# Two attention units share one PSUM tile of two banks, one split per engine and one transpose

## The chip, the core and the metric

The kernel runs on one NeuronCore of a Trainium2 chip. The core has a matrix engine (TensorE, PE in the profile, with its weight loads shown apart as PEld), three engines for elementwise work (VectorE or DVE, ScalarE or ACT, GpSimd or POOL), and SyncE (SP), whose queue issues nearly all DMAs here. Each engine works through its own queue in order and waits at an instruction whose inputs or buffers are not ready. Matmuls write to PSUM, which has eight banks of 512 float32 per partition; DVE and ACT read and write it too. The metric is the device time of one execution in microseconds (us).

## The reference

One layer of an encoder for a sequence of 1024 tokens with 1024 features. One projection of the input gives queries, keys, values and gates of two groups of eight heads of 64 features. Group A is attention in a 2-D neighbourhood of a grid of 16 rows and 64 columns with a learned relative bias; group B is windowed attention with rotary positions, where pairs of query heads share keys and values, and with one more logit per head, the sink. Each group's output is multiplied by SiLU of its gate, projected, added to the scaled input and normalised:

```
h = x @ w_in                                   # 1024 x 1024 by 1024 x 3328
q_a, k_a, v_a, z_a, q_b, k_b, v_b, z_b = split(h)
y_a = neighborhood_attention(q_a, k_a, v_a, rel_bias)      # window 8 x 16
y_b = windowed_gqa_with_sink(rope(q_b), rope(k_b), v_b, sink)   # |i - j| <= 128
mixed = concat(y_a * silu(z_a), y_b * silu(z_b))
x = layer_norm(alpha * x + mixed @ w_out, gain, bias)
```

All is float32 at the outside.

## The kernel before

Float32 products are made from float16 halves: an operand is scaled and split into a high part (a rounding to float16) and a low part (the rest), and three matmuls, high by high, high by low and low by high, stand for one.

The program has three stages. First the values are projected and scales are found. Then the first six of 21 column blocks of the projection run alone (`project`, line 379). In the third stage attention and the other 15 blocks run together: attention goes in steps, and between its matmuls `pump_to` gives out the waiting projection matmuls at a rate that the list `FILL_AT` sets by step. After the last step comes the output projection (`out_mms`, line 1031) and the normalisation.

Attention has 128 units, 64 of group B and then 64 of group A, each 128 queries by up to 384 keys. In group B a unit is a block of 128 queries of one head; the first and last block of a head have 256 keys, the other six 384. In group A a unit is half of the rows of one 16-column strip; its softmax covers 288 or 384 keys (an outer or an inner strip), and the two units of a strip are neighbours. In step i, in the order of the program:

- `stage_qk` (lines 816, 817, 826): two matmuls put the scores of unit i into a bank of PSUM, and one DVE operation adds the bias or mask, finds the row maximum and leaves the negated scores in one of two SBUF buffers.
- `stage_ot` and `stage_pv` (lines 901 and 881), each fourth step: for a quad, four units, probabilities by values, and the transpose of the quad's finished output. The matmuls of quad q come in step 4q + 9.
- `stage_tr` for unit i - 1 (lines 852, 853, 856): ACT writes the high half of the probabilities to an SBUF buffer `split`, DVE the low half, and one DMA issued on SP transposes up to six blocks of 128 by 128 (three blocks of keys, two halves) into a tile `tr`.
- `stage_exp` for unit i (line 842): ACT takes the exponential of the scores into the unit's bank in PSUM and sums each row.

In between, operations that wait in queues of the program's own (`enq`, `pop`: splits of weights, queries and keys, rotary positions, gates) are given out, about one a step for each engine. The order of all engines in this stage is the order in which this code emits (`manual_schedule`).

A unit's bank of PSUM is free for a later unit when the DVE split (line 853) has read it. There are four such banks, taken in turn, two for projection groups ("pj") and two for outputs ("t"). There are six `split` buffers of one unit, used in turn, and nine `tr` tiles of six blocks.

Of the kernel before, what the change touches and what calls it, by code (L numbers as in the profile page):

```python
# [7 lines left out]
F32 = mybir.dt.float32  # L8
F32R = mybir.dt.float32r
F16 = mybir.dt.float16  # L10
I32 = mybir.dt.int32
BF16 = mybir.dt.bfloat16
AF = mybir.ActivationFunctionType
ALU = mybir.AluOpType
# [10 lines left out]
PSCALE = 2.0 ** 14  # L25
MSCALE = 2.0 ** -44
QSCALE = 2.0 ** -15
LTT, LPP, BP, BH, BR, ND, NA, NX, F1 = 1, 6, 2, 9, 5, 1, 1, 6, 0.2
NSPLIT, NP = 6, 2
ORDER = ["zb0", "z0", "zb1", "kb", "qb0", "z1", "qb1", "zb2", "qb2", "k0", "qb3", "zb3", "q0", "k1", "q1",  # L30
         "k2", "q2", "z2", "k3", "q3", "z3"]
NPRO = 6
# [29 lines left out]
def hybrid_block(ctx, tc, xT, x, wt, wv, wo, bias, sink, gain, lbias, cos, sin, bmask, out):  # L62
    nc = tc.nc
    PS = bass.MemoryType.PSUM
# [4 lines left out]
    zp = ctx.enter_context(tc.tile_pool(name="zp", bufs=1))  # L69
    dram = ctx.enter_context(tc.tile_pool(name="dram", bufs=1, space=bass.MemoryType.DRAM))  # L70
    ps2 = ctx.enter_context(tc.tile_pool(name="ps2", bufs=2, space=PS))
    ps1 = ctx.enter_context(tc.tile_pool(name="ps1", bufs=1, space=PS))

    def bank(tag):
        bufs = {"pj": 2, "s": 4, "t": 2}[tag]
        return (ps1 if bufs == 1 else ps2).tile([128, 512], F32, tag=tag, name=f"ps_{tag}", bufs=bufs)

    vd = dram.tile([4, S, 256], F16, name="vd")
    vwin = [dram.tile([4, ROWS, WINW[b] * 256], F16, name=f"vwin{b}") for b in range(4)]
# [10 lines left out]
    for half in range(2):  # L90
        for k in range(KT):
            t = big_tile(f"x{half}{k}", dt=F32 if half else F32R)
# [312 lines left out]
    with ExitStack() as vctx:  # L405
# [4 lines left out]
        ps = bank("t")  # L410
# [154 lines left out]
            nc.vector.tensor_reduce(vm[:, t:t + 1], v32[t], axis=AXX, op=ALU.max, apply_absolute_value=True)  # L565

        tags = ("pj", "pj", "s", "s", "t", "t", "s", "s")
        banks = [bank(t) for t in tags]
        ordered.enter_context(tc.manual_schedule())
        first_tiles()  # L570
        interleave(load_x(0, 1), load_wv(1))
# [43 lines left out]
        ahead(2)  # L615
        v_out(banks[5], 2, 1)
        nc.vector.tensor_mul(vdq, unit[:, 0:1], unit[:, 1:2])
        part = {i: bank(tags[i]) for i in (0, 1, 2, 3, 6, 7)}
        for i, k in enumerate(KO):
            ahead(i + 3)  # L620
            if 1 <= i < 5:
# [24 lines left out]
        for a in range(2):  # L646
            ps = bank(tags[4 + a])
# [106 lines left out]
        return us  # L754

    units = unit_list()
    split = [ap.tile([128, 3, 2, 128], F16, name=f"split{i}", bufs=1) for i in range(NSPLIT)]
    sns = [ap.tile([128, 388], F32, name=f"sn{i}", bufs=1) for i in range(2)]
    for t in split:
        nc.gpsimd.memset(t, 0.0)  # L760
# [2 lines left out]
    st = {}  # L763
    on = {}

    def geom(u):
        g, p, j, t, _ = u
        if g == "a":
            b, half = t
            w = WINW[b]  # L770
            return NKEY[b], [4 * w] * 3
        lo, hi = max(t - 1, 0), min(t + 2, 8)
        return 128 * (hi - lo), [128] * (hi - lo)
# [20 lines left out]
    def stage_qk(u):  # L794
        g, p, j, t, _ = u
        n, _c = geom(u)
        ps = bank("s")
        m, end = n, 384
        if g == "a":
            b, half = t  # L800
            m, end = NROW[half] * WINW[b], 384 if half else 384 - WINW[1]
            q = stks["q", p, j][:, 512 * half + 128 * b:512 * half + 128 * b + 128]
            sl = [stks[w, p, j].rearrange("p (r c) -> p r c", c=GW)[
                :, 4 * half:4 * half + NROW[half], WIN0[b]:WIN0[b] + WINW[b]] for w in ("kh", "kl")]
            bias_t, op = st.pop((u, "b"))
            need(op)
            init = 3e38
        else:
            q = stks["q", f"b{p}", j][:, 128 * t:128 * t + 128]
            lo = max(t - 1, 0) * 128  # L810
            kv = p // 2
            sl = [stks[w, "b", kv][:, lo:lo + n] for w in ("kh", "kl")]
            bias_t = bm[:, 128 if t == 0 else 0:(128 if t == 0 else 0) + n]
            h = 2 * p + j
            init = nsk[:, h:h + 1]
        nc.tensor.matmul(ps[:, :m], q, sl[0], start=True, stop=False)  # L816
        nc.tensor.matmul(ps[:, :m], q, sl[1], start=False, stop=True)  # L817
        s0 = sns[units.index(u) % 2]
        sn = s0[:, end - m:]
        if g == "b" and t < 2:  # L820
            nc.vector.tensor_copy(s0[:, 384:385], nsk[:, h:h + 1])
        elif units.index(u) == 64:
            nc.vector.memset(s0[:, 384 - WINW[1]:384], -NEG)
        nm = ap.tile([128, 1], F32, tag="nm", name="nm", bufs=6)
        c = min(p, 1) if g == "b" else 2
        nc.vector.tensor_tensor_reduce(sn[:, :m], ps[:, :m], bias_t, sg[:, c:c + 1], init,  # L826
                                       op0=ALU.add, op1=ALU.min, accum_out=nm)
        st[u, "sn"] = sn
        st[u, "ps"] = ps
        st[u, "nm"] = nm  # L830

    def stage_exp(u):
        n, _c = geom(u)
        m = n + 1 if u[0] == "b" else n
        sn, nm = st.pop((u, "sn")), st.pop((u, "nm"))
        pt = st.pop((u, "ps"))
        k = units.index(u) % 4
        if k == 0:
            st["sm"] = ap.tile([128, 4], F32, tag="sm", name="sm", bufs=4)
        sm = st["sm"]  # L840
        st[units.index(u) // 4, "sm"] = sm
        nc.scalar.activation(pt[:, :m], sn[:, :m], AF.Exp, bias=nm, scale=-1.0, accum_out=sm[:, k:k + 1])  # L842
        st[u, "p"] = pt

    def stage_tr(u):
        g, p, j, t, _ = u
        n, ch = geom(u)
        pt = st.pop((u, "p"))
        c, m = ch[0], len(ch)
        hl = split[units.index(u) % NSPLIT]  # L850
        src = pt[:, :n].rearrange("p (k c) -> p k c", c=c)
        nc.scalar.activation(hl[:, :m, 0, :c], src, AF.Copy, scale=PSCALE)  # L852
        nc.vector.scalar_tensor_tensor(hl[:, :m, 1, :c], src, PSCALE, hl[:, :m, 0, :c],  # L853
                                       op0=ALU.mult, op1=ALU.subtract)
        tr = ap.tile([128, 6, 128], F16, tag="tr", name="tr", bufs=BH)
        nc.sync.dma_start(tr[:, :2 * m, :], hl[:, :m].rearrange("p k i c -> p (k i c)"), transpose=True)
        st[u, "tr"] = tr

    def quad(q):
        g, p, j, t, _ = units[4 * q]  # L860
# [320 lines left out]
    for i in range(-LD, NU + LO):  # L1181
        if 0 <= i + LD < NU:
            stage_load(units[i + LD], i)
        if i < 0:
            continue
        clock["step"] = i
        per, h = divmod(i, 16)
        bulk["step"] = i
        if i in VA_AT:
            gather_v(0, VA_AT.index(i))  # L1190
        for n, at_ in WO_SCAN:
            if at_ == i:
                load_ops["wo", ("s", n)] = enq("sp", lambda n=n: wo_load(n, True), wo_ops.get(WO_PREV.get(n) if n == 15 else None))
                wo_scan(n, True)
        for n in range(16):
            if WO_LD[n] == i:
                load_ops["wo", n] = enq("sp", lambda n=n: wo_load(n), wo_ops.get(WO_PREV.get(n) if n < 15 else None),
                                        wo_ops.get({9: 0, 10: 1, 12: 2, 13: 3, 14: 4, 15: 5}.get(n)),
                                        w_ops.get(17 + n if 4 <= n <= 8 else None))
                if n < 9 or n == 11:  # L1200
                    wo_scan(n)
        if i == WO_SCALE:
            wo_scale()
        for n in range(len(WO_AT)):
            if WO_AT[n] == i:
                wo_split(n)
        if i == 131:
            enq("sp", gain_load, *m_ops[4])
        if i in M_AT:
            m_queue(4 + M_AT.index(i))  # L1210
        if bulk["last"] != i or (queues["sp"] and i - queues["sp"][0].born > 2):
            pop("sp", 1 if i < 118 else 3)
        if i < NU:
            u = units[i]
            if u[3] in (0, 4):
                need(*stk_ops[f"b{u[1]}", u[2], u[3] // 4])
            if u[3] == (0, 0):
                need(*stk_ops[u[1], u[2], 0], *stk_ops[u[1], u[2], 1])
            stage_qk(u)
        q, m = divmod(i - LP - 3, 4)  # L1220
        if i >= Q30 + 2:
            q, m = (NU // 4 - 2, i - Q30 - 2) if i < Q30 + 4 else divmod(i - LP - 3, 4)
        elif i >= Q30:
            q, m = -1, 0
        if m == 0 and 0 <= q - 1 < NU // 4:
            stage_ot(q - 1)
        if m == 0 and 0 <= q < NU // 4:
            stage_pv(q)
        if i > Z3_END:
            pop("dve", 1, 0)  # L1230
        if 0 <= i - LT < NU:
            stage_tr(units[i - LT])
        pop("act", 1, 0)
        pump_to(i + F1)
        if 0 <= q < NU // 4:
            g, p, j, h = quad(q)
            if g == "a" and p < 3 and (j, h, m) in VA_STEP:
                gather_v(p + 1, VA_STEP.index((j, h, m)))
        if m == 1 and 0 <= q < NU // 4:
            stage_on(q)  # L1240
        pop("dve", ND if i < M_AT[1] else 2, same=True)
        if i < NU:
            stage_exp(units[i])
        pop("act", NA if i < M_AT[0] and len(queues["act"]) < 5 else 2)
        pop("pool", NP)
        pump_to(i + 1)
# [78 lines left out]
```

## Time and profile before

| | us |
|---|---|
| median of 3 runs | 445.71 (445.67 to 446.71) |
| the profiled execution | 446.49 |
| its span, first to last instruction | 444.7 |
| PE, DVE, ACT, POOL busy | 437.5, 344.2, 308.3, 221.6 |
| attention, first to last score matmul | 121.8 to 355.1 |

The page of the profile gives each engine's busy time, the span in 40 slices (tenths of a slice busy, in one digit), the chain of work that ended last, and groups of instructions: line, engine, operation, output and inputs, shape, count, then busy time in us and mean time of one in ns, then the idle time of the engine just before them and what ended it. In a timeline a line begins with the start and the duration in us. In a list of waits the figures are the total in us, the times, and the longest. The end of a matmul is modelled, so its shown duration is longer than the distance to the next one.

### The profile page before, as it was taken

How to read it: one execution, taken by the hardware profiler on the slowest of the kernel's cores; microseconds unless marked ns; L12 is line 12 of the kernel's file. 1: busy time of each engine (PE TensorE's matmuls, PEld its weight loads, DVE VectorE, ACT ScalarE, POOL GpSimd, SP SyncE). 2: the span in 40 equal slices, each digit the busy share in tenths (PEclk: the TensorE clock that was granted, in tenths of full speed). 3: DMA queues.
4: the chain of work that ended last, by engine and by line, in shares of the span. 5: the costliest groups of instructions: out<-in, count | busy, mean ns of one | idle time of the engine just before them, and what ended most of it. 6: DMA issues, size and time to landing. Idle time of an engine off the chain costs nothing.

```text
span 444.7 us, 9505 instructions
## 1 busy us (share of the span) xinstructions
PE 437.5 (98%) x3289; PEld 255.5 (57%) x3289; DVE 344.2 (77%) x849; ACT 308.3 (69%) x700; POOL 221.6 (50%) x235
## 2 busy tenths in 40 slices
PE   9999999999999999999999999999999999999994
PEld 8997754444445565655565655656555654444453
DVE  5978967438986898887988888888878837589944
ACT  5759789766499988887868887888778946302401
POOL 0110074646839558866506767765574405205740
PEclk9999999999999999999999999999999999999997
DMA  8921469984659999587978899998999998103612
GB/s 272 390 91 60 145 235 339 336 292 169 213 127 214 206 190 181 98 162 143 164 127 175 169 182 180 213 170 213 192 204 253 167 172 347 55 0 102 232 69 72
DMA packets 133841, 81.39 MB, mean 183 GB/s; under 512 B 101280, under 2 KB 113440, under 8 KB 133536
## 3 DMA queue, kind: packets, MB, share of 16 engines
q1 hardware_dynamic: 133648, 80.64, 75.4%
q8 instruction: 26, 0.43, 0.4%
q14 instruction: 23, 0.19, 0.2%
q10 hardware_dynamic: 144, 0.13, 0.1%
HBM read 50.34 MB, written 9.96 MB: 136 GB/s over the span
## 4 chain that ended last, share of the span: by engine, by line
PE 91%; DMA 3%; POOL 3%; DVE 1%; issue 1%; ACT 1%; SPq 0%; POOLq 0%; DVEq 0%; ACTq 0%
PE ps_pj L379 44%; PE ps_s L1031 9%; PE ps_s L486 6%; PE ps_t L881 6%; PE ps_pj L1031 5%; PE ps_t L1031 5%; PE ps_s L816 4%; PE ps_s L817 4%; PE ps_pj L486 3%; PE ps_t L486 3%; DMA bias<-in_bias 3%; PE ps_t L901 1%; POOL wl L205 1%; PE ps_t L412 1%; POOL ks L295 1%
## 5 line engine op out<-in xcount | busy, mean ns | idle before, releaser
L379 PE MATMUL ps_pj<-xf,wh 128*128 128x512 f16 x672 | 202.1, 379 | 0.1
L379 PE MATMUL ps_pj<-xf,wl 128*128 128x512 f16 x336 | 127.3, 379 | 0.0
L379 PEld LDWEIGHTS <-wh 128*128 128x128 f16 x672 | 63.7, 98 | 60.4 <-DVE ks L263 0.5
L842 ACT ACTIVATE ps_s<-sn,nm 128x385 f32<-128x385 f32 (+3 forms) x128 | 70.1, 548 | 25.1 <-DVE nm L826 24.6
L853 DVE SCALAR_TENSOR_TENSOR split<-ps_s,split 128x384 f16<-128x384 f32 (+2 forms) x128 | 65.7, 513 | 27.5 <-ACT split L852 25.9
L1031 PEld LDWEIGHTS <-m 128*128 128x128 f16 x432 | 40.0, 98 | 41.1 <-DVE m L939 0.2
L852 ACT ACTIVATE split<-ps_s 128x384 f16<-128x384 f32 (+2 forms) x128 | 57.8, 452 | 2.5 <-DMA tr<-split 0.2
L204 POOL TENSOR_SCALAR wr<-wr,wsc 128x512 f32<-128x512 f32 x26 | 20.6, 791 | 68.1 <-ACT wh L199 61.6
L379 PEld LDWEIGHTS <-wl 128*128 128x128 f16 x336 | 32.9, 98 | 37.4
L826 DVE CUSTOM_DVE_ANT_0 sn<-ps_s,bm,nsk 128x384 f32<-128x384 f32 (+1 forms) x64 | 40.7, 636 | 2.0 <-PE ps_s L817 1.7
L1031 PE MATMUL ps_s<-wo,m 128*128 128x512 f16 (+1 forms) x192 | 40.8, 366 | 0.0
L816 PE MATMUL ps_s<-ks,qs 128*128 128x384 f16 (+4 forms) x128 | 39.2, 306 | 0.3 <-DVE qs L263 0.3
L817 PE MATMUL ps_s<-ks,qs 128*128 128x384 f16 (+4 forms) x128 | 39.2, 306 | 0.0
L826 DVE CUSTOM_DVE_ANT_0 sn<-ps_s,bias,sg 128x264 f32<-128x264 f32 (+1 forms) x64 | 35.0, 547 | 4.5 <-issue 1.5
L881 PEld LDWEIGHTS <-tr 128*128 128x128 f16 (+1 forms) x1104 | 36.6, 98 | 2.2
L205 POOL TENSOR_TENSOR wl<-wr,wh 128x512 f16<-128x512 f32 x26 | 32.7, 1257 | 2.2
L788 POOL TENSOR_SCALAR bias<-bias,rsg 128x552 f32<-128x552 f32 (+1 forms) x24 | 19.1, 797 | 23.8 <-DMA bias<-in_bias 22.6
L295 POOL COPY ks<-ks 64x512 f16<-64x512 f16 x40 | 26.0, 661 | 7.1 <-DVE ks L263 2.8
L1086 ACT ACTIVATE sd<-mv,eps 128x1 f32<-128x1 f32 x8 | 2.4, 295 | 36.5 <-DVE mv L1084 35.2
L1031 PE MATMUL ps_pj<-wo,m 128*128 128x512 f16 (+1 forms) x144 | 26.2, 326 | 0.0
L1130 POOL TENSOR_TENSOR xr<-xr,gb 128x512 f32<-128x512 f32 x7 | 9.8, 1396 | 32.4 <-ACT xr L1127 32.4
L842 ACT ACTIVATION_READ_ACCUMULATOR ps_s<-sn,nm 128x1 f32 x128 | 24.4, 190 | 0.0
(188 smaller groups left out, 813.8 us busy)
## 6 DMA issues: line engine op xcount, KB each, us to landing
ws<-in_wt SPq DMA_DIRECT2D x15, 512.0 KB, 5.9
wr<-in_wt SPq DMA_DIRECT2D x26, 256.0 KB, 3.6
wor<-in_wo SPq DMA_DIRECT2D x22, 256.0 KB, 3.5
bias<-in_bias SPq DMA_DIRECT2D x16, 276.0 KB, 3.3
xr<-in_x SPq DMA_DIRECT2D x8, 512.0 KB, 9.6
out<-xr SPq DMA_DIRECT2D x15, 256.0 KB, 2.1
bias<-in_bias SPq DMA_DIRECT2D x8, 368.0 KB, 3.8
wvraw<-in_wv SPq DMA_DIRECT2D x9, 320.0 KB, 5.8
```

The costliest lines, as they stand in the source:

```text
L205: nc.gpsimd.tensor_sub(l, raw, h)
L295: nc.gpsimd.tensor_copy(t[o, sl], t[a, sl])
L379: nc.tensor.matmul(ps, a[:, k % 4, :], mv, start=(k == 0 and i == 0), stop=(k == KT - 1 and i == 2))
L486: nc.tensor.matmul(ps[:, :320], lh[:, ts], rh[:, cs], start=(k == ko[0] and i == 0), stop=(k == ko[-1] and i == 2))
L816: nc.tensor.matmul(ps[:, :m], q, sl[0], start=True, stop=False)
L817: nc.tensor.matmul(ps[:, :m], q, sl[1], start=False, stop=True)
L826: nc.vector.tensor_tensor_reduce(sn[:, :m], ps[:, :m], bias_t, sg[:, c:c + 1], init, op0=ALU.add, op1=ALU.min, accum_out=nm)
L842: nc.scalar.activation(pt[:, :m], sn[:, :m], AF.Exp, bias=nm, scale=-1.0, accum_out=sm[:, k:k + 1])
L852: nc.scalar.activation(hl[:, :m, 0, :c], src, AF.Copy, scale=PSCALE)
L853: nc.vector.scalar_tensor_tensor(hl[:, :m, 1, :c], src, PSCALE, hl[:, :m, 0, :c], op0=ALU.mult, op1=ALU.subtract)
L881: nc.tensor.matmul(ps[:, HD * m:HD * m + HD], a, b_, start=(i == 0), stop=(i == len(mms) - 1))
L1031: nc.tensor.matmul(ps, lh[:, ts], rh[:, cs], start=(e == EO[0] and i == 0), stop=(e == EO[-1] and i == 2))
```

## The change

Units are taken in pairs, 2k and 2k + 1. A pair has one PSUM tile of two banks, one for each unit, and there are two such tiles in place of four single banks. `stage_tr` runs once for a pair, in step 2k + 2, where it stood for unit 2k + 1 before. Where both units have as many keys, one ACT and one DVE operation split both; where they differ (a first or last block of a head in group B), each unit is split by an operation of its own, and the longer unit is put first. One DMA transposes all blocks of the pair, up to 12. There are three `split` buffers of two units, and four `tr` tiles of 12 blocks. Other users of the tag "s" (the projection of the values, the output projection) take halves of pair tiles.

```diff
-LTT, LPP, BP, BH, BR, ND, NA, NX, F1 = 1, 6, 2, 9, 5, 1, 1, 6, 0.2
-NSPLIT, NP = 6, 2
+LTT, LPP, BP, BH, BR, ND, NA, NX, F1 = 1, 6, 2, 4, 5, 1, 1, 6, 0.2
+NSPLIT, NP = 3, 2
...
+    halves_s = []
+
+    def pair_bank():
+        return ps2.tile([128, 2, 512], F32, tag="s", name="ps_s", bufs=2)
 
     def bank(tag):
-        bufs = {"pj": 2, "s": 4, "t": 2}[tag]
-        return (ps1 if bufs == 1 else ps2).tile([128, 512], F32, tag=tag, name=f"ps_{tag}", bufs=bufs)
+        if tag == "s":
+            if not halves_s:
+                t = pair_bank()
+                halves_s.extend((t[:, 0, :], t[:, 1, :]))
+            return halves_s.pop(0)
+        return ps2.tile([128, 512], F32, tag=tag, name=f"ps_{tag}", bufs=2)
...
-        banks = [bank(t) for t in tags]
+        banks = {i: bank(tags[i]) for i in (0, 1, 2, 6, 3, 7, 4, 5)}
...
-        part = {i: bank(tags[i]) for i in (0, 1, 2, 3, 6, 7)}
+        part = {i: bank(tags[i]) for i in (0, 1, 2, 6, 3, 7)}
...
-    split = [ap.tile([128, 3, 2, 128], F16, name=f"split{i}", bufs=1) for i in range(NSPLIT)]
+    split = [ap.tile([128, 6, 2, 128], F16, name=f"split{i}", bufs=1) for i in range(NSPLIT)]
...
     def stage_qk(u):
...
-        ps = bank("s")
+        if units.index(u) % 2 == 0:
+            halves_s.clear()
+            st["pair"] = pair_bank()
+        ps = st["pair"][:, units.index(u) % 2, :]
...
-    def stage_tr(u):
-        g, p, j, t, _ = u
-        n, ch = geom(u)
-        pt = st.pop((u, "p"))
-        c, m = ch[0], len(ch)
-        hl = split[units.index(u) % NSPLIT]
-        src = pt[:, :n].rearrange("p (k c) -> p k c", c=c)
-        nc.scalar.activation(hl[:, :m, 0, :c], src, AF.Copy, scale=PSCALE)
-        nc.vector.scalar_tensor_tensor(hl[:, :m, 1, :c], src, PSCALE, hl[:, :m, 0, :c],
-                                       op0=ALU.mult, op1=ALU.subtract)
-        tr = ap.tile([128, 6, 128], F16, tag="tr", name="tr", bufs=BH)
-        nc.sync.dma_start(tr[:, :2 * m, :], hl[:, :m].rearrange("p k i c -> p (k i c)"), transpose=True)
-        st[u, "tr"] = tr
+    def stage_tr(k):
+        pt = st.pop((k, "pair"))
+        two = [units[2 * k], units[2 * k + 1]]
+        hl = split[k % NSPLIT]
+        tr = ap.tile([128, 12, 128], F16, tag="tr", name="tr", bufs=BH)
+        sizes = [geom(u) for u in two]
+        if sizes[0] == sizes[1]:
+            n, ch = sizes[0]
+            c, m = ch[0], len(ch)
+            parts_ = [(pt[:, :, :n].rearrange("p u (k c) -> p u k c", c=c),
+                       hl.rearrange("p (u k) i c -> p u k i c", u=2)[:, :, :, :, :c], slice(None))]
+            at_ = (0, 3)
+        else:
+            at_ = (0, 3) if sizes[0][0] > sizes[1][0] else (3, 0)
+            parts_ = []
+            for j in range(2):
+                n, ch = sizes[j]
+                o, m = at_[j], len(ch)
+                parts_.append((pt[:, j, :n].rearrange("p (k c) -> p k c", c=128), hl[:, o:o + m], None))
+        for src, dst, f in parts_:
+            h, l = (dst[:, :, :, 0, :], dst[:, :, :, 1, :]) if f is not None else (dst[:, :, 0, :], dst[:, :, 1, :])
+            nc.scalar.activation(h, src, AF.Copy, scale=PSCALE)
+            nc.vector.scalar_tensor_tensor(l, src, PSCALE, h, op0=ALU.mult, op1=ALU.subtract)
+        w = 2 * (len(sizes[0][1]) + len(sizes[1][1]))
+        nc.sync.dma_start(tr[:, :w, :], hl.rearrange("p k i c -> p (k i c)")[:, :128 * w], transpose=True)
+        for j in range(2):
+            st[two[j], "tr"] = tr[:, 2 * at_[j]:]
...
-        if 0 <= i - LT < NU:
-            stage_tr(units[i - LT])
+        if 0 <= i - LT < NU and (i - LT) % 2 == 1:
+            stage_tr((i - LT) // 2)
```

More of the change, by code (lines that the diff above doesn't have):

```diff
@@ L71, in hybrid_block @@
     ps2 = ctx.enter_context(tc.tile_pool(name="ps2", bufs=2, space=PS))
-    ps1 = ctx.enter_context(tc.tile_pool(name="ps1", bufs=1, space=PS))
+    halves_s = []
+    def pair_bank():
+        return ps2.tile([128, 2, 512], F32, tag="s", name="ps_s", bufs=2)
     def bank(tag):
-        bufs = {"pj": 2, "s": 4, "t": 2}[tag]
-        return (ps1 if bufs == 1 else ps2).tile([128, 512], F32, tag=tag, name=f"ps_{tag}", bufs=bufs)
+        if tag == "s":
[4 more added lines that the diff above has]
+        return ps2.tile([128, 512], F32, tag=tag, name=f"ps_{tag}", bufs=2)
     vd = dram.tile([4, S, 256], F16, name="vd")
@@ L829, in stage_qk @@
         st[u, "ps"] = ps
+        st[units.index(u) // 2, "pair"] = st["pair"]
         st[u, "nm"] = nm
@@ L842, in stage_exp @@
         nc.scalar.activation(pt[:, :m], sn[:, :m], AF.Exp, bias=nm, scale=-1.0, accum_out=sm[:, k:k + 1])
-        st[u, "p"] = pt
-    def stage_tr(u):
-        g, p, j, t, _ = u
-        n, ch = geom(u)
-        pt = st.pop((u, "p"))
-        c, m = ch[0], len(ch)
-        hl = split[units.index(u) % NSPLIT]
-        src = pt[:, :n].rearrange("p (k c) -> p k c", c=c)
-        nc.scalar.activation(hl[:, :m, 0, :c], src, AF.Copy, scale=PSCALE)
-        nc.vector.scalar_tensor_tensor(hl[:, :m, 1, :c], src, PSCALE, hl[:, :m, 0, :c],
-                                       op0=ALU.mult, op1=ALU.subtract)
-        tr = ap.tile([128, 6, 128], F16, tag="tr", name="tr", bufs=BH)
-        nc.sync.dma_start(tr[:, :2 * m, :], hl[:, :m].rearrange("p k i c -> p (k i c)"), transpose=True)
-        st[u, "tr"] = tr
+    def stage_tr(k):
[25 more added lines that the diff above has]
+            st[two[j], "tr"] = tr[:, 2 * at_[j]:]
     def quad(q):
```

## The prediction

> **What bounds the kernel now.** I read the page from the top: engine shares, slices, the chain that ended last. Then I asked the waits of PE alone, the matmul spacing, and the busy time in the attention stretch.
>
> ```profile
> span 444.7 us, 9505 instructions
> PE 437.5 (98%) x3289; PEld 255.5 (57%) x3289; DVE 344.2 (77%) x849; ACT 308.3 (69%) x700; POOL 221.6 (50%) x235
> PE   9999999999999999999999999999999999999994
> PE 91%; DMA 3%; POOL 3%; DVE 1%; issue 1%; ACT 1%; SPq 0%; POOLq 0%; DVEq 0%; ACTq 0%
> ```
>
> ```profile
> PE ps_t L1111 <- ACT dr L1109: 1.8, 1, 1.8
> PE ps_t L412 <- DVE warm L127: 1.0, 1, 1.0
> PE ps_s L816 <- DVE qs L263: 0.3, 1, 0.3
> ```
>
> ```profile
> 68.72 10.38 PE ps_pj L379 x48
> 160.35 1.29 PE ps_pj L379 x6
> ```
>
> ```profile
> 121.70:355.00 233.30, 232.94 (x2086) 133.84 (x2084) 194.73 (x546) 193.21 (x494) 146.79 (x163) 1.00 0.93 178
> ```
>
> TensorE is busy in every slice and is 91% of the chain. Its only wait inside attention is 0.3 us; the others stand at the start (1.0) and in the last row's norm (1.8). The busy figure is a modelled one, so I checked it by spacing: 48 projection matmuls take 10.38 us where no attention runs (216 ns each), and 6 take 1.29 us in the middle of it (215 ns). There is no hidden slack. The last row (columns PE, PEld, DVE, ACT, POOL) says that in the 233.3 us of attention PE idles 0.4 us, while DVE is busy 83% and ACT 83%. So a shorter ACT or DVE operation is worth nothing by itself; a new wait on PE is worth its full length, since PE has no idle time later in which to make it good.
>
> The Trainium skill (Perfetto Trace Analysis, Identifying the Most-Contended Engine) says matmul busy share is a poor measure of the distance to roofline and that the LDWEIGHTS share should be read. By it the 57% of PEld would leave PE much room, and relieving ACT and DVE could gain. The equal spacing of the two L379 rows speaks against that here, so I leave the gain a small chance only.
>
> **The change part by part.** The durations:
>
> ```profile
> L852 ACT ACTIVATE split<-ps_s 128x384 f16<-128x384 f32 x80 | 38.7, 483 | 1.3
> L852 ACT ACTIVATE split<-ps_s 128x288 f16<-128x288 f32 x32 | 13.1, 408 | 0.9 <-DMA tr<-split 0.2
> L852 ACT ACTIVATE split<-ps_s 128x256 f16<-128x256 f32 x16 | 6.1, 381 | 0.4
> L853 DVE SCALAR_TENSOR_TENSOR split<-ps_s,split 128x384 f16<-128x384 f32 x80 | 44.4, 555 | 18.4 <-ACT split L852 17.2 <-POOL wl L205 0.4
> L853 DVE SCALAR_TENSOR_TENSOR split<-ps_s,split 128x256 f16<-128x256 f32 x16 | 6.7, 422 | 2.6 <-ACT split L852 2.4
> L826 DVE CUSTOM_DVE_ANT_0 sn<-ps_s,bm,nsk 128x384 f32<-128x384 f32 x48 | 32.1, 670 | 1.9 <-PE ps_s L817 1.7
> L842 ACT ACTIVATE ps_s<-sn,nm 128x385 f32<-128x385 f32 x48 | 27.9, 582 | 5.5 <-DVE nm L826 5.3
> L842 ACT ACTIVATION_READ_ACCUMULATOR ps_s<-sn,nm 128x1 f32 x128 | 24.4, 190 | 0.0
> L856 SPq DMA_TRANSPOSE tr<-split x128: 1188/1212/2615, 126.1 to 361.3; - x128
> DMA to landing us min/median/max: 2.5/3.4/6.2
> 139.14 1.19 SPq L856 DMA_TRANSPOSE tr<-split  x1
> ```
>
> *Merged splits, work removed.* From 256 to 384 columns L852 grows by 102 ns (0.80 ns a column, fixed part 0.18 us), L853 by 133 ns (1.04 ns, fixed 0.16). Of the 64 pairs, 48 have equal sizes and merge (16 of group b, 32 of group a); the 16 pairs with an edge block still take two operations on each engine. Removed: 48 x 0.18 = 8.5 us of ACT, 48 x 0.16 = 7.5 us of DVE. Both lie beside PE: counted 0.
>
> *Merged splits, delay added.* One L852 of 768 columns takes 0.79 us (estimate from that line), L853 0.95. The split of the odd unit of a pair, which stood at the same place in both queues, so ends later by 0.31 + 0.40 = 0.71 us in a 384 pair, by 0.23 + 0.30 = 0.53 in a 288 pair. In an edge pair the other unit's split stands ahead: 0.28 us later where the small block is first, 0.58 where it is last. Behind the longer L852 waits the exponential of the next unit, behind L853 the next score reduction; both shift by the same.
>
> *Two slots in place of four banks.* Before, the score matmul of unit u+4 waited for the split of unit u. Now the first matmul of pair k+2, that is of unit 2k+4, waits for the split of unit 2k+1: one unit less of run-ahead. Queued behind it on PE is everything (projection, PV). The margin is read from before: start of L816 of unit u+3 minus end of L853 of odd unit u. First of the 62 margins short against the added delay (u=5), the worst of four crowded stretches (u=13, 45, 63, 85), the last short one (u=93), and one from between two stretches (u=23, third pair of lines):
>
> ```profile
> 133.37 0.56 DVE L853 SCALAR_TENSOR_TENSOR split<-ps_s,split 128x384 f16<-128x384 f32 x1
> 134.51 0.27 PE L816 MATMUL ps_s<-ks,qs 128*128 128x256 f16 x1
> 148.52 0.56 DVE L853 SCALAR_TENSOR_TENSOR split<-ps_s,split 128x384 f16<-128x384 f32 x1 [1.06 <-ACT split L852]
> 147.89 0.27 PE L816 MATMUL ps_s<-ks,qs 128*128 128x256 f16 x1
> 164.78 0.43 DVE L853 SCALAR_TENSOR_TENSOR split<-ps_s,split 128x256 f16<-128x256 f32 x1
> 167.53 0.33 PE L816 MATMUL ps_s<-ks,qs 128*128 128x384 f16 x1
> 207.79 0.55 DVE L853 SCALAR_TENSOR_TENSOR split<-ps_s,split 128x384 f16<-128x384 f32 x1
> 208.32 0.27 PE L816 MATMUL ps_s<-ks,qs 128*128 128x256 f16 x1
> 242.41 0.42 DVE L853 SCALAR_TENSOR_TENSOR split<-ps_s,split 128x256 f16<-128x256 f32 x1
> 241.29 0.31 PE L816 MATMUL ps_s<-ks,qs 128*128 128x352 f16 x1
> 284.06 0.56 DVE L853 SCALAR_TENSOR_TENSOR split<-ps_s,split 128x384 f16<-128x384 f32 x1 [0.64 <-ACT split L852]
> 283.97 0.28 PE L816 MATMUL ps_s<-ks,qs 128*128 128x264 f16 x1
> 299.14 0.56 DVE L853 SCALAR_TENSOR_TENSOR split<-ps_s,split 128x384 f16<-128x384 f32 x1 [0.48 <-ACT split L852]
> 299.06 0.28 PE L816 MATMUL ps_s<-ks,qs 128*128 128x264 f16 x1
> ```
>
> Margins: 134.51 - 133.93 = 0.58; 147.89 - 149.08 = -1.19; between the stretches 167.53 - 165.21 = 2.32; then -0.02; -1.54; -0.65; -0.64. Less the added delay (0.71; edge pair at u=63: 0.58) those of u=5, 13, 45, 63, 85 and 93 are short by 0.1, 1.9, 0.7, 2.1, 1.4 and 1.35 us. At u=23 DVE and ACT have caught up, so a wait in one does not pay for the next. If a wait pays for the rest of its stretch, PE loses 1.9 + 0.7 + 2.1 + 1.4 = **6.1 us**. If every short pair pays anew, the 29 shortfalls of the same kind (0.1 the first, 1.35 the last) add up to **22 us**. Lower end: the 0.16 us that a merged pair saves, over some three merged pairs ahead of each worst point, gives 0.5 us back four times: 4 us; and if DVE and ACT catch up faster than that, 0. I take 6.1 plus a fifth of the other 16, **+9.3 us**: nearer the lower row, since a PE that has waited is later for its neighbours too, but not at it, because the queue around each pair becomes longer. That loop runs from one L853 to the next: L853, next odd unit's L826, L842 with its accumulator read, L852. Before 0.56 + 0.67 + 0.08 + 0.58 + 0.19 + 0.48 = 2.56 us for two units, after 0.95 + 1.52 + 0.79 = 3.26, against 2 x 1.84 us of PE (units 0 to 127 start between 121.77 and 355.07):
>
> ```profile
> L826 DVE DVE_READ_ACCUMULATOR2_ANT nm<- 128x1 f32 x128 | 10.6, 83 | 0.0
> 121.77 0.27 PE L816 MATMUL ps_s<-ks,qs 128*128 128x256 f16 x1
> 355.07 0.29 PE L816 MATMUL ps_s<-ks,qs 128*128 128x288 f16 x1
> ```
>
> Where one queued filler operation of 0.4 us or more falls into the loop, the pair runs slower than PE.
>
> The Trainium skill (Perfetto Trace Analysis, Optimizing Scalar/DVE Operations) says larger operations help an engine that is saturated, and that where Scalar and Vector are not saturated but cause bubbles on others, breaking operations up may finish sooner. With both 83% busy the rule speaks against this change; the sum by it has the same sign as mine.
>
> *One transpose for two units.* 64 issues fewer on SP. The eighth, with 4 blocks, took 1.19 us, the median of mostly 6-block ones 1.21, so an issue hardly grows with blocks: 12 should take between 1.2 and 2.4, and I take 1.3, which frees some 70 us of SP. The loads queued there (weights, bias, values) come earlier or equal; PE waits for none, so 0. Even units are transposed one step later; PV starts only after the last unit of its quad, whose place is unchanged. Landing: 3.4 us now; between 3.4 and 6.8 for twice the blocks, I take 4.6. What covers it is the distance to PV, priced below as a rival; 0 in the sum.
>
> *Buffers.* Four transposed tiles of 12 blocks and three split buffers for two units keep the reuse distances (8 units against 9, and 6). The order of banks in the V projection makes three tiles there share a release; their copies end before PE returns to them: 0. In the output projection halves of a pair are taken in turn; their readers are done long before: 0.
>
> Sum: 446.49 (the profiled execution: span 444.7 and 1.8 around it) + 9.3 = 455.8; that run is 0.78 over the median 445.71, so **455.0 us**.
>
> **The rivals.**
>
> *PE does not stall (not slower).* The place is the release at unit 63, short by 2.1 us. It decides if DVE and ACT arrive there 2.1 us earlier, that is if the saved 0.16 and 0.18 us per merged pair and the halved number of hand-overs (17.2 us of idle time of the 384 form of L853 ends with L852) add up over the 16 merged pairs before it instead of being used up by idle time. For it: 16 x 0.16 = 2.6 us. Against: margins of over 2 us between the stretches say that savings do not carry over. Time 445.7; a true gain is bounded by PE's 0.4 us of idle time in attention.
>
> *Every pair pays.* The loop of 3.26 us plus filler is longer than 3.67 us nearly throughout; the 22 us above: 468 us.
>
> *The transpose lands late.* Unit 59:
>
> ```profile
> 235.52 1.21 SPq L856 DMA_TRANSPOSE tr<-split  x1
> 239.04 0.75 PE L881 MATMUL ps_t<-vb,tr 128*128 128x64 f16 x20
> ```
>
> 235.52 + 3.4 = 238.9, and PV starts at 239.04, reaching this unit's matmuls some 0.7 us later. With 0.71 us of later split and 1.2 us of longer landing that quad is short by 1.1; at a landing of 6.8 us it is short by 3.3. From unit 59's score matmul to its PV lie six steps, so lateness that lasts stretches all 128 units by a sixth of it: 1 us of it costs 21 us. It decides at a landing over about 5 us. Against it: SP's backlog shrinks, and unit 59 is among the tightest. Time with 0.5 us lasting: 466.
>
> *The two halves are not independent.* If the second half's matmul waited for the first half's reduction and exponential, each pair would cost 0.67 + 0.08 + 0.58 + 0.19 = 1.5 us: +97, 542 us. Each half is a bank of its own and has its own writer, so this is unlikely.
>
> **How the numbers follow.** Stalls in the crowded stretches, 450 to 460 us: 0.60. Every pair pays: 0.14. Late landing: 0.07. Dependent halves: 0.02. No stall, within 0.3% (1.3 us, about what a measurement of this kernel can tell from no change): 0.13. Faster: 0.04. The slower cases hold 0.83. The range 446 to 467 leaves out the gain, part of no change, and the upper half of the last three, about 0.2.
>
> **What would show it.** Right: PE waits of L816 on L853, 4 to 20 us, first near units 13 to 17 and again near unit 63; L853 of 768 columns near 0.95 us, 48 times; L856 64 times near 1.3 us; DVE and ACT busy less by 7 to 9 us; PE's spacing otherwise unchanged. Wrong: no L816 wait (first rival); waits of L881 on the transpose (landing); L816 waiting for L826 or L842 of the other half (halves); or a merged operation far from its line.

## The result, and the profile after

The changed kernel takes 511.21 us (median of 6 runs, 507.33 to 512.55), the kernel before 445.91 us beside it (6 runs): a ratio of 1.145 with a 95% interval of 1.141 to 1.149, or 65 us more. The forecast was 455.0, with a range to 467. Among the six runs the time goes with the granted clock of TensorE: two at a mean of 0.994 took 507.3 and 509.0 us, two at 0.984 took 512.4 and 512.6, so some 4 of the 65 us may be the clock's.

The page of the changed kernel: span, engines, slices of PE, chain, and the groups that answer to those shown of before. Behind the second bar of a group stands the engine's idle time just before it.

```profile
span 510.5 us, 9166 instructions
...
PE 452.6 (89%) x3289; PEld 257.7 (50%) x3289; DVE 345.9 (68%) x801; ACT 306.1 (60%) x652; POOL 221.0 (43%) x232
...
PE   9999999998768878887877889899988989999995
...
PE 21%; POOL 7%; issue 6%; ACT 5%; DVE 5%; DMA 3%; SPq 1%; POOLq 0%; DVEq 0%; ACTq 0%
...
L827 PE MATMUL ps_s<-ks,qs 128*128 128x384 f16 (+4 forms) x128 | 39.4, 308 | 50.8 <-ACT ps_s L854 40.6
```

PE does the same 3289 matmuls, but from the tenth slice on it is no longer busy throughout, and the chain that was 91% PE now passes from engine to engine (the shares listed for it add up to about half of the span, so part of it is not accounted for). L827 is the first of the two score matmuls of a unit (L816 before). In front of it PE is idle 50.8 us, where before it was 0.3 us. The waits of PE, in the changed kernel (total us, times, longest):

```profile
PE ps_s L827 <- ACT ps_s L854: 40.6, 46, 2.2
PE ps_s L827 <- DVE sn L832: 6.0, 4, 2.2
PE ps_s L827 <- DVE split L878: 3.7, 4, 0.9
```

L854 is the exponential of a unit that is at most one step older. Such a unit has nothing to give to a score matmul, unless it is the other half of the same PSUM tile. One place in the timeline of PE, and the same of ACT, shows that it is. The unit at 192.96 is the even one of its pair, that at 194.97 the odd one:

```profile
192.96 0.33 PE L827 MATMUL ps_s<-ks,qs 128*128 128x384 f16 x1
...
194.37 0.38 PE L387 MATMUL ps_pj<-xf,wl 128*128 128x512 f16 x1
194.97 0.27 PE L827 MATMUL ps_s<-ks,qs 128*128 128x256 f16 x1 [0.23 <-ACT ps_s L854]
```

```profile
193.30 0.81 ACT L877 ACTIVATE split<-ps_s 128x768 f16<-128x768 f32 x1
194.21 0.59 ACT L854 ACTIVATE ps_s<-sn,nm 128x385 f32<-128x385 f32 x1
194.73 0.19 ACT L854 ACTIVATION_READ_ACCUMULATOR ps_s<-sn,nm 128x1 f32 x1
```

The even unit's exponential ends with its accumulator read at 194.73 + 0.19 = 194.92, and the odd unit's matmul starts 0.05 us later. The exponential writes 385 of the 512 columns of its half, the matmul the other half. That is so in all 64 pairs: the odd unit's first matmul starts 0.05 us after that read ends, also where the list shows no idle time because the modelled end of the matmul before covers it. Some of the waits that the list puts down to L832 or L878 ended with such a read too. By the starts of the matmuls alone (216 ns for one of 512 columns) PE loses about 60 us at 61 places ahead of the L827 of an odd unit, and 0.6 us at two places ahead of that of an even one; the kernel before loses 0.4 us at one.

How far the score matmuls stand apart says it in another way. The means are over all 128 starts, the first at 121.89 and the last at 420.12 in the changed kernel:

| mean distance, us | even to odd unit of a pair | odd unit to the next pair |
|---|---|---|
| before | 1.55 | 2.13 |
| changed | 2.51 | 2.19 |

The first column grows by 0.96 us, over 64 pairs 61 us; the second by 0.06, over 63 distances 4 us. Nearly all of the loss lies inside the pair.

Two more views of the changed kernel bear on the forecast's terms: the attention stretch (PE, PEld, DVE, ACT and POOL busy, granted clock, DMA share, GB/s), and the transposes.

```profile
122.50:425.00 302.50, 251.66 (x2136) 138.12 (x2135) 199.00 (x507) 195.46 (x457) 146.18 (x162) 0.98 0.71 140
```

```profile
L880 SPq DMA_TRANSPOSE tr<-split x64: 1253/1430/2537, 129.6 to 423.5; - x64
...
DMA to landing us min/median/max: 3.3/3.7/6.6
```

DVE and ACT, which were busy 83% of the stretch, are now busy 66% and 65%: neither is overloaded, they wait in a circle with PE.

### The profile page after: what moved, and what is told of

It is laid out like the page before. It is cut to its first block, busy times and chain, and to the rows that moved or that the text cites. A ratio compares the mean times of both kernels' runs of the same rounds, so it can differ in the third digit from the quotient of the medians.

```text
span 510.5 us, 9166 instructions
## 1 busy us (share of the span) xinstructions
PE 452.6 (89%) x3289; PEld 257.7 (50%) x3289; DVE 345.9 (68%) x801; ACT 306.1 (60%) x652; POOL 221.0 (43%) x232
## 5 line engine op out<-in xcount | busy, mean ns | idle before, releaser
L387 PE MATMUL ps_pj<-xf,wh 128*128 128x512 f16 x672 | 204.9, 384 | 0.0
L854 ACT ACTIVATE ps_s<-sn,nm 128x385 f32<-128x385 f32 (+3 forms) x128 | 70.3, 549 | 73.6 <-DVE nm L837 73.0
L827 PE MATMUL ps_s<-ks,qs 128*128 128x384 f16 (+4 forms) x128 | 39.4, 308 | 50.8 <-ACT ps_s L854 40.6
L878 DVE SCALAR_TENSOR_TENSOR split<-ps_s,split 128x768 f16<-128x768 f32 (+3 forms) x80 | 58.3, 729 | 31.1 <-ACT split L877 30.2
L837 DVE CUSTOM_DVE_ANT_0 sn<-ps_s,bm,nsk 128x384 f32<-128x384 f32 (+1 forms) x64 | 41.0, 641 | 33.4 <-PE ps_s L828 27.0
L877 ACT ACTIVATE split<-ps_s 128x768 f16<-128x768 f32 (+3 forms) x80 | 49.8, 623 | 17.5 <-DVE split L878 16.3
L837 DVE CUSTOM_DVE_ANT_0 sn<-ps_s,bias,sg 128x264 f32<-128x264 f32 (+1 forms) x64 | 35.2, 551 | 32.6 <-issue 12.3
L828 PEld LDWEIGHTS <-qs 128*128 128x128 f16 x128 | 12.5, 98 | 73.1 <-issue 65.6
L212 POOL TENSOR_SCALAR ws<-ws,wsc 128x512 f32<-128x512 f32 x16 | 11.1, 692 | 31.2 <-ACT wh L207 30.8
```

Source lines behind the costliest of these rows:

```text
L212: nc.gpsimd.tensor_scalar(raw, raw, scale, 1.0, op0=ALU.mult, op1=ALU.mult)
L387: nc.tensor.matmul(ps, a[:, k % 4, :], mv, start=(k == 0 and i == 0), stop=(k == KT - 1 and i == 2))
L877: nc.scalar.activation(h, src, AF.Copy, scale=PSCALE)
L878: nc.vector.scalar_tensor_tensor(l, src, PSCALE, h, op0=ALU.mult, op1=ALU.subtract)
```

## The experiments

Theory after the result: the program's waits tie the two halves of a tile (the rival "the two halves are not independent"). Rivals: the late split and release (the forecast's own term), the merged operations, and the joint transpose. The pieces of code are shortened: `...` stands for what is left out, and comments in them are added here.

**One bank for each unit.** The changed kernel with four single banks: two splits on each engine per pair, at the place of the joint one, and one transpose of up to 12 blocks.

```diff
-        if units.index(u) % 2 == 0:
-            halves_s.clear()
-            st["pair"] = pair_bank()
-        ps = st["pair"][:, units.index(u) % 2, :]
+        ps = bank("s")                     # 4 single banks
...
+        for src, h, l in parts_:           # one entry for each unit
             nc.scalar.activation(h, src, AF.Copy, scale=PSCALE)
+        for src, h, l in parts_:
             nc.vector.scalar_tensor_tensor(l, src, PSCALE, h, op0=ALU.mult, op1=ALU.subtract)
```

> The changed kernel with four single banks in place of the two pair tiles: each unit has its own PSUM tile and its own ACT and DVE split, but both are still split in step 2k+2 and leave in one transpose of 12 blocks, with the same buffers. Theory A (in a pair tile the second unit's score matmul waits for the first unit's exponential; in the changed kernel it starts 0.05 us after that exponential's end in every one of the 64 pairs): the waits of PE on ACT go, 445 to 455 us. Theory B (release in pairs and the longer loop of the prediction): the splits are as late as in the changed kernel and banks of a pair come free together, so most of the loss stays, over 480 us. Theory C (12 blocks land late): the transposes are unchanged, so about 511 us.

Measured: 454.16 us beside 446.22 of the kernel before, a ratio of 1.017 (1.016 to 1.019). The even-to-odd distance is back at 1.56 us; the other is 2.24, 0.11 above the kernel before, over 63 distances 7 us. PE's longest wait (in its list of waits) is the one that the forecast named:

```profile
PE ps_s L819 <- DVE split L863: 3.6, 8, 1.2
```

57 of the 65 us are gone with the pair tile and the merged operations; the kernels below tell which of the two. What is left, 7.9 us, shows mostly as the late release: by the starts of the matmuls PE loses 8.2 us ahead of L819, of which the list puts 1.2 down to a rotary operation on POOL and 1.1 to queries that DVE splits.

**The pair tile alone.** The kernel before, with nothing changed but the PSUM tiles; splits and transposes are a unit's own and at their old places.

```diff
+        if units.index(u) % 2 == 0:
+            halves_s.clear()
+            st["pair"] = pair_bank()
+        ps = st["pair"][:, units.index(u) % 2, :]
-        ps = bank("s")
```

> The kernel before with nothing changed but the PSUM tiles: two pair tiles in place of four single banks; splits, transposes and buffers for each unit as before. Theory A: the second unit's matmul waits for the first unit's exponential in all 64 pairs, and the second exponential also for the first unit's split by DVE: 500 us or more. Theory B: a pair's release is later by one unit only, with short splits: 446 to 455 us. Theory C: 446 us.

Measured: 523.5 us, a ratio of 1.174 (1.171 to 1.176), more than the whole change. The waits of PE and then those of ACT in this kernel:

```profile
PE ps_s L827 <- ACT ps_s L853: 61.5, 63, 2.7
```

```profile
ACT split L863 <- DVE nm L837: 68.0, 56, 2.6
...
ACT ps_s L853 <- DVE split L864: 27.3, 52, 0.7
```

The tile makes the loss without any merged operation. The ties show on ACT too: the split of one unit waits for the score reduction (L837) of the other half, and the exponential for the other half's split (L864). In 62 of the 64 pairs the even unit's split by ACT starts 0.03 to 0.04 us after the odd unit's reduction ends, though both operations only read the tile. So the tie is not one of writes alone.

**Both units' score matmuls first.** The changed kernel with its pair tiles and merged operations, but with the odd unit's two matmuls put right behind the even unit's, so that no exponential stands between them. In a second kernel the odd unit's reduction on DVE is moved with them.

```diff
-            stage_qk(u)
+            if i % 2 == 0:
+                stage_qk(u, True)              # the two matmuls only
+                stage_qk(units[i + 1], True)
+            stage_qk(u, False)                 # the reduction
```

```diff
-            stage_qk(u, False)
+                stage_qk(u, False)
+                stage_qk(units[i + 1], False)
```

> The changed kernel with only the second unit's two score matmuls moved, right behind the first unit's, in step 2k. Its reduction by DVE and its exponential stay in step 2k+1. Theory A: PE no longer waits for the exponential; the second unit's reduction on DVE may still wait for it, which costs PE nothing directly: 450 to 475 us. Theory B and C: unchanged splits and transposes, about 511 us.

> As the run before, with the second unit's reduction moved too, so that both reductions stand before both exponentials: no operation on one half stands between two on the other but on its own engine. Theory A: all waits between halves are gone from PE, 446 to 462 us, and not slower than the run before. Theory B: the loop of split, reduction, exponential and split stays; over 480 us. Theory C: about 511 us.

Measured: 480.11 us, a ratio of 1.075 (1.074 to 1.077), for the matmuls alone; 462.75 us, 1.038 (1.035 to 1.041), with the reduction. PE's waits in the first and in the second, then ACT's in the second:

```profile
PE ps_s L829 <- DVE split L881: 18.8, 26, 1.7
```

```profile
PE ps_s L829 <- DVE split L881: 10.6, 15, 2.0
```

```profile
ACT split L880 <- DVE split L881: 19.1, 16, 2.8
```

The first lies above the 450 to 475 us expected, the second just above its 462. In the first kernel the odd unit's reduction still stands a step later, behind the even unit's exponential, which writes to the tile that it reads; in none of the 64 pairs does it start before that exponential has ended, where in the kernel before it does in 28. So the tie only moves on to DVE, and the pair's split and its release come late, which does cost PE. With both stages moved, no wait on an exponential is left on PE, and 48 us of the loss are gone though the tile is still a shared one. So the cost is not the shared tile itself, but an order in which another engine's operation on one half stands between two operations on the other.

The last line shows a second tie of the same kind. In the 16 pairs of unequal units, ACT's second split waits for DVE's first one, which reads and writes the same `split` buffer in another place. The changed kernel has it too:

```profile
ACT split L877 <- DVE split L878: 16.3, 16, 2.7
```

**High halves first.** As the second of these, and in the unequal pairs both splits on ACT are emitted before both on DVE.

```diff
-        for src, dst, f in parts_:
-            h, l = ...
+        for (src, dst, f), (h, l) in zip(parts_, hls):
             nc.scalar.activation(h, src, AF.Copy, scale=PSCALE)
+        for (src, dst, f), (h, l) in zip(parts_, hls):
             nc.vector.scalar_tensor_tensor(l, src, PSCALE, h, op0=ALU.mult, op1=ALU.subtract)
```

> The run with both score matmuls and both reductions first (462.8 us), with the operations of the 16 unequal pairs in another order: both high splits on ACT, then both low splits on DVE. There ACT waited 19 us in 16 places for the first unit's low split before it began the second unit's high split, which lies in the same buffer tile. If that wait between halves lies on PE's path too, 456 to 460 us; if not, 462 to 463.

Measured: 454.89 us beside 446.89 of the kernel before, a ratio of 1.018 (1.015 to 1.021), a little below the 456 to 460 expected. Engines, and PE's wait for the pair's release:

```profile
PE 438.3 (97%) x3289; PEld 254.5 (56%) x3289; DVE 339.6 (75%) x801; ACT 303.0 (67%) x652; POOL 220.4 (49%) x232
```

```profile
PE ps_s L829 <- DVE split L883: 4.3, 6, 1.6
```

This kernel has all parts of the change, pair tile, merged splits, joint transpose, and no tie that PE waits for. By the three ratios, each against the kernel before on its own chip, the loss splits into 0.107 for the tie inside the pair (1.145 - 1.038; 48 us), 0.020 for the second tie (9 us) and 0.018 for the rest (8 us). These shares hold for this order of taking the ties out and are not parts that add up: in the changed kernel nearly all of the loss stands ahead of odd units, since a PE that waits there loses little to a late release, and the pair tile alone loses 77 us. This kernel stands beside the first experiment, which has the same late split without merged operations and without pair tiles, and with the stages of a pair in their old order: 1.018 and 1.017. So the merged operations bring nothing that the time shows.

**The transpose alone, and the late split alone.** The first is the kernel before with each unit's split at its old place and one transpose for two units. The second is the first experiment (late splits, single banks) with a transpose for each unit.

```diff
-        hl = split[units.index(u) % NSPLIT]
+        k, x = divmod(units.index(u), 2)
+        hl = split[k % NSPLIT]             # a unit's own half, o = 0 or 3
...
+        if x == 0:
+            return
+        tr = ap.tile([128, 12, 128], F16, tag="tr", name="tr", bufs=BH)
+        w = 2 * (len(sizes[0][1]) + len(sizes[1][1]))
+        nc.sync.dma_start(tr[:, :w, :], hl.rearrange("p k i c -> p (k i c)")[:, :128 * w], transpose=True)
```

```diff
-        nc.sync.dma_start(tr[:, :w, :], hl.rearrange("p k i c -> p (k i c)")[:, :128 * w], transpose=True)
         for j in range(2):
+            o, m = at_[j], len(sizes[j][1])
+            nc.sync.dma_start(tr[:, 2 * o:2 * o + 2 * m, :], hl[:, o:o + m].rearrange("p k i c -> p (k i c)"), transpose=True)
```

> The kernel before with only the transposes and their buffers changed: single banks, each unit split at its old place by operations of its own, then one transpose of 12 blocks for a pair in step 2k+2, three split buffers of two units and four transposed tiles. If the 8.0 us that the run with single banks and late splits still loses come from the splits (releases), this is 446 us, the same as before; if they come from the transpose or its buffers, about 454 us.

> The run with single banks and late splits (454.2 us), with a transpose for each unit in place of one for the pair. If the splits alone cost the 8 us: 453 to 455 us, with PE's waits on the low split unchanged. If the joint transpose costs: 446 to 448 us.

Measured: 445.70 us (12 runs) beside 446.89 (17 runs), a ratio of 0.997 (0.996 to 0.998), for the transpose alone; 454.60, a ratio of 1.017 (1.015 to 1.020), for the late split alone. Page, PE's wait in attention and the transposes (count, median us from issue to landing) of the first:

```profile
span 443.4 us, 9244 instructions
...
PE 436.8 (99%) x3289; PEld 255.0 (58%) x3289; DVE 344.2 (78%) x849; ACT 307.6 (69%) x700; POOL 222.0 (50%) x232
```

```profile
PE ps_s L816 <- DVE qs L263: 0.3, 1, 0.3
```

```profile
tr<-split SPq DMA_TRANSPOSE x64, 4.0
```

PE's waits in the second:

```profile
PE ps_s L819 <- DVE split L863: 4.2, 8, 1.2
PE ps_t L891 <- DMA tr<-split: 2.6, 4, 1.0
```

The joint transpose costs nothing. The late split makes the whole of the last 8 us, with the joint transpose (1.017) or without it (1.017). The transpose alone is the fastest of the changed kernels. Its gain of 0.3% lies at the bound of what can be told: PE's waits are those of the kernel before, and the kernel before ran at 445.9 to 446.9 in its three groups, nearly the same difference. I take it as no loss and a possible small gain, not as a gain that is shown.

## Why the prediction was wrong

The failing step is the last rival and its chance: "Each half is a bank of its own and has its own writer, so this is unlikely", at 0.02. Where the bank stands is not what counts. The waits that the program carries go by the tile, and the two halves of a tile were tied by them in 64 of 64 pairs. The prediction had named the sign of it, L816 waiting for L842 of the other half; that is the main wait after. Two banks as such need no such wait: in the kernel before, 47 of the 128 score matmuls start while an exponential is being written to another bank, and 63 of the 64 odd units' matmuls start before the even unit's exponential has ended. Units 22 and 23 there, a pair after the change:

```profile
161.21 0.59 ACT L842 ACTIVATE ps_s<-sn,nm 128x385 f32<-128x385 f32 x1
161.49 0.27 PE L816 MATMUL ps_s<-ks,qs 128*128 128x256 f16 x1
```

A kernel with two banks in one tile and without the wait was not run. The tie on the shared `split` buffer, the second tie above, is in no term of the prediction.

*The price of that rival.* It was 1.5 us a pair, 97 in all; the distance in a pair grew by 0.96 us, 61 in all. Two errors in it work against each other, so that the price came near is in part luck. The sum set the whole chain down as a loss, though PE has other work between the two units, 1.55 us of it before: what counts is how much longer the chain is than that. And the chain was taken too short, as reduction and exponential alone. Measured from the even matmul to the odd one it has a mean of 2.51 us: 0.68 to the start of the reduction, 0.60 for the reduction, 0.52 until ACT begins the exponential, 0.67 for that, 0.05 to the odd matmul. In the place shown it is 194.97 - 192.96 = 2.01 us, as ACT is free there when the reduction ends. At 37 of the other places the exponential stands behind the split of the pair before (L877), 30 us in all. With 1.5 for the chain and 1.55 taken off, no loss would have come out.

*Late release, +9.3 us.* Right in mechanism and place, and near in size, for what the change is without the ties. The three kernels with late splits and no tie that PE waits for give 1.017, 1.017 and 1.018; that is 7.9 us in the first experiment. The forecast put the first wait near units 13 to 17. In the first experiment it is the row that follows, unit 16. Its bank is a single one, and it starts 0.05 us after the first of the pair's two splits ends, that of unit 12; unit 13, the other of that pair, was the first of the forecast's four worst points. There 1.9 us were forecast and 1.17 measured. The longest of the other losses that a late split explains stand ahead of units 60 and 88, near the forecast's points 63 and 85. At unit 48, behind point 45, PE waits 1.2 us, which the list puts down to the operation on POOL there, and to the split in the kernel with a transpose for each unit. The lower end (0) and "every pair pays" (+22 us) both fall.

```profile
150.21 0.27 PE L819 MATMUL ps_s<-ks,qs 128*128 128x256 f16 x1 [1.17 <-DVE split L863]
```

*Merged splits.* The saving was taken too large. Groups by form of the changed kernel:

```profile
L878 DVE SCALAR_TENSOR_TENSOR split<-ps_s,split 128x768 f16<-128x768 f32 x32 | 30.6, 956 | 14.5 <-ACT split L877 13.7 <-POOL wr L212 0.6
...
L877 ACT ACTIVATE split<-ps_s 128x768 f16<-128x768 f32 x32 | 25.6, 800 | 0.5
```

0.96 and 0.80 us, where the forecast had 0.95 and 0.79. All splits together went from 57.9 to 49.8 us on ACT (38.7 + 13.1 + 6.1 before), 8.1 less for a forecast of 8.5. But the busy time of the whole engine fell by only 2.2 us on ACT (308.3 to 306.1) and rose on DVE by 1.7, in place of the 7 to 9 less that I had named; in the kernel without ties it fell by 5.3 and 4.6. The rows explain it: one instruction's row often begins before the row ahead of it ends (194.73 against 194.21 + 0.59 above), and the engine's busy time counts that stretch once. Added up over the 200 largest groups, the rows fell from 343.1 to 335.2 us on ACT and from 379.6 to 373.7 on DVE, but they also overlap less. So the fixed part of a row is not what a merged operation saves. The first experiment has the two splits of a pair one right behind the other:

```profile
149.09 0.85 ACT L861 ACTIVATE split<-ps_s 128x384 f16<-128x384 f32 x2
149.60 1.02 DVE L863 SCALAR_TENSOR_TENSOR split<-ps_s,split 128x384 f16<-128x384 f32 x2 [1.20 <-ACT split L861]
```

Two separate splits take 0.85 and 1.02 us, a merged one 0.80 and 0.96: it saves 0.05 and 0.06 us, a third of the 0.18 and 0.16 of the forecast. That it is worth nothing to the time was right. By the Trainium skill (Perfetto Trace Analysis, Optimizing Scalar/DVE Operations), smaller operations may let work end sooner where Scalar and Vector aren't saturated but cause bubbles on other engines. Here smaller ones (first experiment) and larger ones (high halves first) gave the same 1.017 and 1.018, so no run shows it for this kernel.

*Transposes.* The issue has a median of 1.43 us (1.3 forecast, between 1.2 and 2.4), the landing 3.7 us in the changed kernel, 3.8 in the first experiment and 4.0 in the transpose alone (4.6 forecast). The rival of a late landing falls: in the kernels with a joint transpose PE waits for it once at most, 1.0 us, and the one with a transpose for each unit, which shows more (2.6 us in 4 waits, quoted above), takes as long as the first experiment.

*The cost of nothing for the moved even unit and the buffers* holds: the transpose alone, with three split buffers and four transposed tiles, loses nothing.

## What to carry to other kernels

A tile is also the unit of this program's waits: before two producers are put into one tile, list every operation that touches it, reads too, and ask whether, in the order in which the operations are emitted, another engine's operation on one half stands between two on the other. If so, either keep two tiles, or emit a pair's matmuls, then its reductions, then its exponentials, as the kernels here did which won 48 us back. Price a new wait by the whole chain, with its hand-overs and the work queued ahead, minus what the waiting engine does meanwhile, and test a joint design part by part: here the part that cost nothing (the joint transpose) needed none of the parts that cost 65 us.

## What was unexpected of the hardware

A DMA transpose's issue hardly depends on its size: 1.19 us for 4 blocks and a median of 1.21 for mostly 6 in the kernel before, 1.43 (1.25 at least) for up to 12, so that two units in one transpose free about 1 us of SP's queue. Its landing grows by 0.3 to 0.6 us only (a median of 3.4, and 3.7 to 4.0) for twice the blocks. And the granted clock of the stalling kernel was lower in the profiled execution, 0.98 in attention against 1.00 there in the kernel before, the first experiment, high halves first and the transpose alone, whose PE hardly waits; why is open.
